# One decoder layer on one core: the feed-forward's way down as a plain product by token quarters, a new order of gate/up, and a new start

## The chip, the cores and the metric

The kernel runs on one core of one Trainium2 chip. The metric is device time in microseconds for one execution; the time of a kernel is the median of its runs. A profiled execution is one more run, recorded by the hardware profiler; its span is what the trace covers.

## The reference

One step of a hybrid decoder, one layer (DEPTH = 1), in fp32. 1024 prompt tokens and 8 x 8 sample tokens share the weights; D_MODEL is 1024 and FFN_HIDDEN 2816. What matters here, cut from the reference:

```python
def rmsnorm(x, g):
    xf = x.astype(jnp.float32)
    y = xf * lax.rsqrt(jnp.mean(xf * xf, axis=-1, keepdims=True) + EPS)
    return (y * g.astype(jnp.float32)).astype(x.dtype)

def swiglu(xn, w_gate, w_up, w_down):
    g = jnp.einsum('btd,df->btf', xn, w_gate)
    u = jnp.einsum('btd,df->btf', xn, w_up)
    return jnp.einsum('btf,fd->btd', jax.nn.silu(g) * u, w_down)

# per layer, for the prompt (yp) and the sample tokens (ys):
#   project_mixers(rmsnorm(yp, g_mix), w_in, ...) -> window attention and mLSTM -> w_out, added to yp
#   yp = yp + cross_attend(rmsnorm(yp, g_cross), ...)
yp = yp + swiglu(rmsnorm(yp, g_ffn[l]), w_gate[l], w_up[l], w_down[l])
ys = ys + swiglu(rmsnorm(ys, g_ffn[l]), w_gate[l], w_up[l], w_down[l])
y_prompt = rmsnorm(yp, g_final)
```

## The kernel before

**Layout and number form.** All 1088 tokens lie as columns, features on the 128 partitions. Every fp32 operand is split into a high and a low part (`split`, and for weights `prep`): a copy to fp32r on ScalarE (ACT) gives the high part, a subtraction on VectorE (DVE) the low one. A product is three matmuls (`mm3`, recorded under line 92): high by high, low by high, high by low. So one weight block of 128 x 128 against one column group makes three matmuls.

**The start.** The x tiles (8 tiles of 128 x 1088) are loaded one after the other on SyncE's queue (SP), split into `xhi` and `xlo` (L116, L117) by ACT or DVE in turn, and squared for the norm (L210). The first two output tiles of the input projection (`win_f[0]`, `win_f[1]`, weights `whi`, `wlo`) run tile by tile as x arrives; their accumulators are `sc`, `o` and `mm`. Then `pt<-sq,ones` sums the squares over the partitions with plain fp32 products, and the products of the token-major weights `win_a` (`wthi`, `wtlo`) follow.

**The feed-forward part** is the last one. Tokens form two halves z of 544 columns; each product has 272 columns. The hidden width is 22 tiles, in 11 pairs `p`. Gate/up (`gate_up`) makes, for each pair and each of the two matrices, a 2 x 2 block product in seven products in place of eight: x is held as `Operand`s (four block pairs, with sums made by `fill`, splits on ACT and DVE, the additions on POOL for z = 0 and on DVE for z = 1), and the weights come as four blocks and four sums of blocks. Each of the seven products of a pair takes one weight `wo` (2 x 512 columns, four blocks of 128) and runs 12 matmuls for each half. Results are combined by `keep` (copy to `kp` on ACT, L1202) and additions and multiplications into `h` on DVE (L1229, L1232, L1233), and `h` is stored to DRAM (`hd`) on POOL's queue.

The first 6 pairs (`NU = 6`) run for z = 0 alone and, much later, for z = 1 alone. Their block sums `sgu` were made ahead of time by DRAM-to-DRAM copies and accumulating copies, spread over earlier parts (`presum`). The last 5 pairs run for both halves together; their block sums `ws` are made by DVE (`sums`, L1131 to L1134). In the same part `dn_sums` makes the block sums of all 11 pairs of down's weights `wdn` on DVE and stores them to DRAM (`sdn`) on POOL's queue.

Down is also a seven-product block product. It goes in six groups of three or four pairs (`downs`), between which the z = 1 runs of pairs 0 to 5 stand (`second`). Each group loads the hidden tiles back from DRAM (`load_h`, `hb<-hd`, 544 KB each) and makes an `Operand` of each. Results are added into `yy` (L1281), which holds the layer's input; `Final` makes squares and their sums, the norm, the last scaling (L1321) and the stores.

**What sets the order.** `all_ops` is the list of all weights in the order of their use; `raw` loads each (`wr`, six buffers) on SP's queue, `prep` splits it (`wo`, five buffers; L1182 on ACT, L1183 on DVE), one weight ahead of its use. A scheduler merges the engines' instructions; on each engine they run in order, so an instruction that waits holds everything behind it on its engine. POOL's queue carries the stores and loads of hidden tiles, of `yy` and of `sdn`. A slot (`slot(tag, ...)`) is reused when its last reader is done.

Of the kernel before, what the change touches and what calls it, by code (L numbers as in the profile page):

```python
# [15 lines left out]
P = 128  # L16
# [9 lines left out]
NU = 6  # L26
# [3 lines left out]
EPS = 1e-6  # L30
NEG = -1.0e30
# [14 lines left out]
def tile_hymba_step(  # L46
# [56 lines left out]

    def gcol(base, k):
        return vv[:, base + k:base + k + 1]


    def split(hi, lo, src, scale=None, eng=None):
# [3 lines left out]
        else:  # L112
            if eng is V:
                V.tensor_scalar_mul(hi, src, scale)
            else:
                A.activation(hi, src, AF.Copy, scale=scale)  # L116
            V.scalar_tensor_tensor(lo, src, scale, hi.bitcast(F32), ALU.mult, ALU.subtract)  # L117

# [75 lines left out]
    xs, xr = [], []  # L194
    for k in range(NK):
        xr.append(slot("cm"[k % 2], [T], name="xraw"))
        nc.sync.dma_start(xr[k], xT[k])
# [4 lines left out]
        if k == 0:  # L202
            w = load_w(win_f[0], NK)
        if k == 0:
            w1 = load_w(win_f[1], NK)
# [56 lines left out]
    def tok_w(src, n, per, tags):  # L262
        parts = []
        for k0 in range(0, NK, per):
            tag = tags[k0 // per]
            raw = wp.tile([P, per, n], F32, tag="wraw", name="wrawt", bufs=2)
            nc.sync.dma_start(raw, src[:, k0:k0 + per, :])
            hi, lo = slot(tag[0], [per, n], F32R, name="wthi"), slot(tag[-1], [per, n], F32R, name="wtlo")
            split(hi, lo, raw)
            parts.append((hi, lo))  # L270
        return lambda k: (parts[k // per][0][:, k % per, :], parts[k // per][1][:, k % per, :])

# [10 lines left out]
    wa = tok_w(win_a, 264, 4, "qm")  # L283
# [12 lines left out]
    for b in range(NB + 1):  # L296
# [4 lines left out]
        if b == NB:  # L301
            next(presum)
# [310 lines left out]
    for blk in range(NB):  # L613
# [25 lines left out]
        if blk % 3 == 1:  # L639
            next(presum)  # L640
# [217 lines left out]
    for u in range(2 * NB):  # L858
# [3 lines left out]
        if u % 3 == 0:  # L862
            next(presum)
# [161 lines left out]
    class Operand:  # L1025
# [14 lines left out]
        def fill(self, b, a, eng=V):  # L1040
            def part(hi, lo, src, scale=None):
# [5 lines left out]
            part(self.b[:, 0:2], self.s_, b)  # L1047
            eng.tensor_tensor(a[:, 0], a[:, 0], a[:, 1], ALU.subtract)
# [6 lines left out]
            return self  # L1055
# [4 lines left out]
    def x_part(z):  # L1060
# [6 lines left out]
        xo[z].append(Operand(xt[z], xo[z][-1] if j % 2 else None).fill(b, a, V if z else G))  # L1067
# [32 lines left out]
    x_part(0)  # L1100
    x_part(0)
# [13 lines left out]
    sdn = dr.tile([NP2, P, 4, 512], F32, name="sdn")  # L1115
# [37 lines left out]
    def dn_ops(g):  # L1153
        for src, i in ((wdn, 0), (wdn, 1), (sdn, 0), (sdn, 1), (sdn, 2), (sdn, 3), (wdn, 3)):
            for p in g:
                yield raw(src[p, :, i, :])


    downs = [(0, (0, 1, 2, 3)), (0, (4, 5, 6, 7)), (0, (8, 9, 10)),
             (1, (7, 8, 9, 10)), (1, (6, 0, 1, 2)), (1, (3, 4, 5))]  # L1160

    second = [(0,), (1,), (2,), (3, 4), (5,), ()]

    def all_ops():
        for p in range(NU):
            yield from gu_ops(p)
        dn = iter(range(NP2))
        for p in range(NU, NP2):
            yield from gu_ops(p)
            for _ in range(3 if p == NP2 - 1 else 2):  # L1170
                dn_sums(next(dn))
        for us, (z, g) in zip(second, downs):
            for p in us:
                yield from gu_ops(p)
            yield from dn_ops(g)
# [335 lines left out]
```

## Time and profile before

| what | us |
|---|---|
| three runs | 1395.67, 1395.81, 1399.73 |
| median | 1395.81 |
| the profiled execution | 1392.54 |
| its span | 1390.70 |
| feed-forward part in it | 604.3 to 1376 |
| TensorE busy | 1288.6 (93%) |
| DVE busy | 939.1 (68%) |
| ACT busy | 684.4 (49%) |
| POOL busy | 187.3 (13%) |

Matmuls are pipelined: a record lasts longer than the distance to the next one, so the cost of a product is read from starts, or from a stretch without gaps. Idle time of an engine other than TensorE costs something only where TensorE waits for that engine.

### The profile page before, as it was taken

Reading aid. Unit: us, or ns where it says so; the run is one execution under the profiler, and the core shown is the slowest. Engines: PE = TensorE matmul, PEld = TensorE weight load, DVE = VectorE, ACT = ScalarE, POOL = GpSimd, SP = SyncE. Lnnn points to the kernel's source line nnn. Section 1 sums busy time; section 2 is a strip of 40 time slices with the busy share of each in tenths; the row PEclk is TensorE's granted clock in tenths of the full one; section 3 lists DMA queues with packets and bytes.
Section 4 is the critical chain, followed back from the end, with each engine's and each line's share of the span. In section 5 each row is a group of like instructions: output and inputs, shape, how many; then the busy total and the mean of one; then the engine's idle time right before and its main releaser. Section 6 shows DMA issues by size and latency. Waiting matters only on the chain.

```text
span 1390.7 us, 24905 instructions
## 1 busy us (share of the span) xinstructions
PE 1288.6 (93%) x9194; PEld 1199.5 (86%) x9194; DVE 939.1 (68%) x2120; ACT 684.4 (49%) x1579; POOL 187.3 (13%) x234
## 2 busy tenths in 40 slices
PE   7999999999999899959999999999798999798996
PEld 6999888887888787759999999999798999798995
DVE  7224345467766677799766665666778798868887
ACT  4322233457654566567654333333555467546553
POOL 2000111200003551350000111112100000200000
PEclk9999999999999999979999999999899999999998
DMA  5123443547763753536764555556756675875663
GB/s 224 38 75 92 145 116 108 135 97 145 241 122 91 197 123 105 176 128 219 241 208 133 184 166 175 166 176 234 248 175 207 188 222 156 289 225 167 200 185 106
DMA packets 108435, 230.44 MB, mean 166 GB/s; under 512 B 13730, under 2 KB 19298, under 8 KB 108314
## 3 DMA queue, kind: packets, MB, share of 16 engines
q1 hardware_dynamic: 82713, 156.50, 36.1%
q0 software_dynamic: 19264, 59.78, 15.8%
q10 hardware_dynamic: 6336, 12.58, 3.0%
q8 instruction: 72, 1.18, 0.4%
q14 instruction: 50, 0.40, 0.1%
HBM read 193.18 MB, written 60.80 MB: 183 GB/s over the span
## 4 chain that ended last, share of the span: by engine, by line
PE 27%; issue 18%; DVE 8%; DMA 4%; POOL 2%; ACT 2%; POOLq 0%; DVEq 0%; SPq 0%; ACTq 0%
PE b L92 25%; POOL sdn L1151 2%; DMA wr<-sgu 1%; DVE wo L1183 1%; DVE bl L111 1%; DVE yy L1321 1%; PE mm L92 1%; DMA wr<-wgu 1%; DMA sdn<-ws 1%; PE sc L92 1%; PE o L92 1%; DMA hb<-hd 0%; DVE bl L117 0%; DVE bs L111 0%; DVE y L1066 0%
## 5 line engine op out<-in xcount | busy, mean ns | idle before, releaser
L92 PE MATMUL b<-bh,wo 128*128 128x272 f32 x2112 | 421.7, 293 | 29.1 <-DVE kp L1232 13.5
L92 PEld LDWEIGHTS b<-bh,wo 128*128 128x128 f32 x2112 | 342.1, 191 | 35.6 <-DVE kp L1232 16.0
L92 PE MATMUL b<-bb,wo 128*128 128x272 f32 x1848 | 322.8, 295 | 23.2 <-DVE wo L1183 10.8
L1183 DVE TENSOR_TENSOR wo<-wr,wo 128x512 fp32r<-128x512 f32 x352 | 238.5, 692 | 105.1 <-ACT wo L1182 105.0
L92 PE MATMUL b<-bl,wo 128*128 128x272 f32 x1056 | 307.7, 291 | 0.0
L1182 ACT ACTIVATE wo<-wr 128x512 fp32r<-128x512 f32 x352 | 218.9, 628 | 169.5 <-PE b L92 117.8
L92 PEld LDWEIGHTS b<-bb,wo 128*128 128x128 f32 x1848 | 277.6, 193 | 27.9 <-DVE wo L1183 12.4
L92 PEld LDWEIGHTS b<-bl,wo 128*128 128x128 f32 x1056 | 201.9, 191 | 0.1
L92 PE MATMUL b<-bs,wo 128*128 128x272 f32 x528 | 153.9, 291 | 0.0
L92 PEld LDWEIGHTS b<-bs,wo 128*128 128x128 f32 x528 | 101.1, 192 | 0.0
L92 PE MATMUL mm<-xlo,whi 128*128 128x384 f32 (+1 forms) x288 | 97.9, 340 | 0.0
L92 PE MATMUL mm<-xhi,whi 128*128 128x384 f32 (+1 forms) x288 | 97.8, 340 | 0.0
L92 PE MATMUL mm<-xhi,wlo 128*128 128x384 f32 (+1 forms) x288 | 96.7, 336 | 0.0
L1202 ACT ACTIVATE kp<-b 128x272 f32<-128x272 f32 x132 | 51.8, 394 | 86.1 <-PE b L92 86.1
L1281 DVE TENSOR_TENSOR yy<-yy,b 128x272 f32<-128x272 f32 x168 | 64.8, 436 | 12.9 <-PE b L92 12.6
L110 ACT ACTIVATE whi<-wraw 128x1024 fp32r<-128x1024 f32 x39 | 41.1, 1055 | 59.5 <-PE mm L92 51.4
L92 PE MATMUL mm<-chi,wlo 128*128 128x384 f32 (+1 forms) x192 | 64.5, 336 | 1.2 <-POOL wlo L111 1.1
L92 PE MATMUL mm<-chi,whi 128*128 128x384 f32 (+1 forms) x192 | 65.2, 340 | 0.0
L92 PE MATMUL mm<-clo,whi 128*128 128x384 f32 (+1 forms) x192 | 63.6, 331 | 0.0
L92 PEld LDWEIGHTS mm<-xhi,whi 128*128 128x128 f32 x288 | 54.8, 190 | 3.1 <-issue 1.8
L92 PEld LDWEIGHTS mm<-xlo,whi 128*128 128x128 f32 x288 | 54.9, 191 | 2.9 <-issue 1.3
L92 PEld LDWEIGHTS mm<-xhi,wlo 128*128 128x128 f32 x288 | 55.0, 191 | 1.5 <-issue 0.9
(390 smaller groups left out, 2242.6 us busy)
## 6 DMA issues: line engine op xcount, KB each, us to landing
wr<-wgu SPq DMA_DIRECT2D x112, 256.0 KB
wr<-wdn SPq DMA_DIRECT2D x110, 256.0 KB
wr<-sgu SPq DMA_DIRECT2D x96, 256.0 KB
wr<-sdn SPq DMA_DIRECT2D x88, 256.0 KB
sgu<-wgu ACTq DMA_DIRECT2D x12, 1024.0 KB
hd<-h POOLq DMA_DIRECT2D x22, 544.0 KB, 4.4
hb<-hd POOLq DMA_DIRECT2D x22, 544.0 KB, 4.8
sdn<-ws POOLq DMA_DIRECT2D x44, 256.0 KB, 5.4
```

Source lines behind the costliest of these rows:

```text
L92: return TE.matmul(out, lhsT, rhs, start=start, stop=stop, skip_group_check=skip)
L110: A.activation(hi, src, AF.Copy)
L111: (eng or V).tensor_tensor(lo, src, hi.bitcast(F32), ALU.subtract)
L1151: G.dma_start(sdn[p, :, i, :], t)
L1182: A.activation(w[:, 0], t, AF.Copy)
L1183: V.tensor_tensor(w[:, 1], t, w[:, 0].bitcast(F32), ALU.subtract)
L1202: A.activation(t, src, AF.Copy)
L1281: V.tensor_tensor(v, v, b[dp], op)
L1321: V.scalar_tensor_tensor(v, v, gcol(V_FIN, 2 * dp + i), r, ALU.mult, ALU.mult)
```

## The change

**The feed-forward part.** `NU` is 4. The order is: pairs 0 to 3 for z = 0 alone, pairs 4 to 10 for both halves, pairs 0 to 3 for z = 1 alone, and then all of down. Down is a plain product, in four token quarters (z, q) of 272 columns: for each of four pairs of output tiles, 22 hidden tiles are accumulated in two banks by 11 weights of 4 blocks, 44 weights a quarter. `wdn` is laid out on the host in this order. No sums of down's weights are made or stored. `hidden` loads the 11 tiles of a quarter from `hd` (272 KB each, in pieces of 1088 bytes, on POOL's queue) into raw slots and splits each once into `hhl`; those of the next quarter are made during the current one. One more weight is prepared ahead (an extra `prep()`). The first two `x_part(0)` calls are cut in two by a `yield`, and the additions of all parts go to DVE. `yy` of z = 1 has slots of its own.

**The start.** Eleven products of a 128 x 128 fp32 tile of zeros with itself go first on TensorE. The first weight and the first x tile are loaded in pieces, the first two weights are split by DVE alone, all x tiles have their high part from ACT. The squares come behind the split of the last x tile, their sums go to DVE alone, and `tok_w(win_a)` is called ahead of the first products.

```diff
-NU = 6
+NU = 4
+IDLE = 11
+    idle = tmp([P], name="idle")
+    V.memset(idle, 0.0)
+    rest = ops([P])
+    for _ in range(IDLE):
+        mm(rest, idle, idle)
...
+    def split_w(raw, parts):
...
+        for k0, k1 in parts:
+            V.tensor_copy(hi[:, k0:k1, :], raw[:, k0:k1, :])
+            V.tensor_tensor(lo[:, k0:k1, :], raw[:, k0:k1, :], hi[:, k0:k1, :].bitcast(F32), ALU.subtract)
...
-        split(hi, lo, xr[k], gcol(V_MIX, k), V if k % 2 else A)
+        if k == 0:
+            raw = first_w(0)
+            nc.sync.dma_start(raw[:, 0:2, :], win_f[0][:, 0:2, :])
+            nc.sync.dma_start(xr[k][:, 0:CH[0][1]], xT[k][:, 0:CH[0][1]])
+            nc.sync.dma_start(xr[k][:, CH[0][1]:T], xT[k][:, CH[0][1]:T])
+            nc.sync.dma_start(raw[:, 2:NK, :], win_f[0][:, 2:NK, :])
+            raw1 = first_w(1)
+            nc.sync.dma_start(raw1, win_f[1])
+            w = split_w(raw, ((0, 2), (2, NK)))
+            for c0, c1 in (CH[0], (CH[0][1], T)):
+                split(hi[:, c0:c1], lo[:, c0:c1], xr[k][:, c0:c1], gcol(V_MIX, k), A)
+            w1 = split_w(raw1, ((0, 2), (2, NK)))
+        else:
+            nc.sync.dma_start(xr[k], xT[k])
+            x_done = split(hi, lo, xr[k], gcol(V_MIX, k), A)
...
-        A.activation(sq, xr[k], AF.Square)
+        with tc.issue_after(x_done.ins):
+            A.activation(sq, xr[k], AF.Square)
...
-            (G if k < 4 else V).tensor_tensor(sums[-1], sums[-1], sq, ALU.add)
+            V.tensor_tensor(sums[-1], sums[-1], sq, ALU.add)
...
+    wa = tok_w(win_a, 264, 4, "qm")
...
-    def dn_sums(p):
-        for i, t in enumerate(sums(*[raw(wdn[p, :, i, :]) for i in range(4)])):
-            G.dma_start(sdn[p, :, i, :], t)
...
     def all_ops():
+        for p in range(NP2):
+            yield from gu_ops(p)
         for p in range(NU):
             yield from gu_ops(p)
...
+        for _ in range(4):
+            for dp in range(4):
+                for i in range(NP2):
+                    yield raw(wdn[dp, i])
...
+    def hidden(z, q):
+
+        hs = [None] * NP2
+
+        def step(p0):
+            n = min(2, NP2 - p0)
+            t = slot("q", [2, 2, HC], name="hraw")
+            for i in range(n):
+                nc.gpsimd.dma_start(t[:, i], hd[z, p0 + i].rearrange("p (a q) c -> p q a c", q=2)[:, q])
+            for i in range(n):
+                o = slot(HT[q][p0 + i], [4, HC], F32R, name="hhl")
+                split(o[:, 0:2], o[:, 2:4], t[:, i])
+                hs[p0 + i] = o
+        return hs, [lambda p0=p0: step(p0) for p0 in range(0, NP2, 2)]
...
+        for dp in range(4):
+            acc = [bank(4 * (dp % 2) + i) for i in range(2)]
+            for i in range(NP2):
                 w = next_w()
+                for j in range(4):
+                    dd, k = divmod(4 * i + j, FT)
+                    o, e = hs[k // 2], k % 2
+                    mm3(acc[dd], w[:, 0, j * P:j * P + P], w[:, 1, j * P:j * P + P],
+                        o[:, e], o[:, 2 + e], k == 0, k == FT - 1)
+                    if k == FT - 1:
+                        v = yy[z][dp][:, dd, q * HC:q * HC + HC]
+                        V.tensor_tensor(v, v, acc[dd], ALU.add)
+                        fin[z].add(2 * dp + dd, q)
...
+    hs, steps = hidden(0, 0)
+    for p in range(NU):
+        gate_up(p, (1,), {1: own if p == 0 else slot("m", [4, HC], name="h")},
+                [lambda: None] * 4 + steps if p == 1 else ())
+    load_yy(1)
...
+    quarters = [(0, 0), (0, 1), (1, 0), (1, 1)]
+    for i, (z, q) in enumerate(quarters):
+        nx_hs, steps = hidden(*quarters[i + 1]) if i < 3 else (None, ())
+        down(z, q, hs, steps)
+        hs = nx_hs
```

TensorE at the program's start; `sc`, `o` are accumulators, `idle` the tile of zeros. Before:

```order
L1507 UNCONDITIONAL_BRANCH
L92 MATMUL sc_171<-xhi_89,whi_95 128x384
L92 MATMUL sc_171<-xlo_90,whi_95 128x384
L92 MATMUL sc_172<-xhi_89,whi_95 128x384
L92 MATMUL sc_171<-xhi_89,wlo_96 128x384
```

And now:

```order
L1514 UNCONDITIONAL_BRANCH
L93 MATMUL o_87<-idle_85 128x128 x11
L93 MATMUL sc_205<-xhi_102,whi_111 128x384
L93 MATMUL sc_205<-xlo_103,whi_111 128x384
L93 MATMUL sc_205<-xhi_102,wlo_112 128x384
```

The eleven zero products stand ahead of the first product with data.

DVE in the part with both halves. Lines 1131 to 1134 of before and 1167 to 1170 of after are block sums of weights: `ws_8945` to `ws_8948` and `ws_8965` to `ws_8968` are sums of `wdn` blocks, `ws_7934` to `ws_7937` of gate/up's blocks. `wo` is a weight's low part, `kp` and `h` belong to the results. Before:

```order
L1183 TENSOR_TENSOR wo_8811<-ws_8772,wo_8811 128x512
L1132 TENSOR_TENSOR ws_8946<-ws_8945,wr_8937 128x512
L1133 TENSOR_TENSOR ws_8947<-wr_8937,wr_8941 128x512
L1183 TENSOR_TENSOR wo_8844<-ws_8774,wo_8844 128x512
L1134 TENSOR_TENSOR ws_8948<-wr_8939,ws_8946 128x512
L1131 TENSOR_TENSOR ws_8965<-wr_8961,wr_8963 128x512
L1132 TENSOR_TENSOR ws_8966<-ws_8965,wr_8957 128x512
L1183 TENSOR_TENSOR wo_8875<-ws_8775,wo_8875 128x512
L1232 TENSOR_TENSOR kp_8754<-b_8770,kp_8754 128x272
```

And now:

```order
L1168 TENSOR_TENSOR ws_7935<-ws_7934,wr_7852 128x512
L1201 TENSOR_TENSOR wo_7757<-ws_7687,wo_7757 128x512
L1169 TENSOR_TENSOR ws_7936<-wr_7852,wr_7856 128x512
L1201 TENSOR_TENSOR wo_7790<-ws_7688,wo_7790 128x512
L1250 TENSOR_TENSOR kp_7708<-b_7724,kp_7708 128x272
L1170 TENSOR_TENSOR ws_7937<-wr_7854,ws_7935 128x512
L1251 SCALAR_TENSOR_TENSOR h_7444<-kp_7708,h_7444 128x272
```

The sums of `wdn` blocks no longer stand among the low parts and results of gate/up; its own sums do.

ACT where the part with both halves ends. `hb` are hidden tiles loaded for a seven-product group, `bb` and `bh` parts of their operands, `hraw` hidden tiles loaded for a quarter, `hhl` their split parts. Before:

```order
L1182 ACTIVATE wo_10595<-wr_10593 128x512
L1182 ACTIVATE wo_10633<-wr_10631 128x512
L110 ACTIVATE bb_10614<-hb_10087 128x272
L110 ACTIVATE bb_10614<-hb_10087 128x544
L1182 ACTIVATE wo_10669<-wr_10667 128x512
L110 ACTIVATE bh_10612<-hb_10087 128x544
L110 ACTIVATE bb_10652<-hb_10130 128x272
```

And now:

```order
L1200 ACTIVATE wo_10797<-wr_10795 128x512
L1200 ACTIVATE wo_10817<-wr_10815 128x512
L117 ACTIVATE hhl_11167<-hraw_11164 128x544
L117 ACTIVATE hhl_11170<-hraw_11164 128x544
L1200 ACTIVATE wo_10836<-wr_10834 128x512
L117 ACTIVATE hhl_11195<-hraw_11192 128x544
L1220 ACTIVATE kp_10812<-b_10794 128x272
L1200 ACTIVATE wo_10856<-wr_10854 128x512
```

Two splits of one raw tile stand between weight copies where four parts of an operand stood.

## Rows read from the trace of the kernel before

**Rows 1.** The page's busy times: engine, us, share of the span, instructions.

```profile
PE 1288.6 (93%) x9194; PEld 1199.5 (86%) x9194; DVE 939.1 (68%) x2120; ACT 684.4 (49%) x1579; POOL 187.3 (13%) x234
```

**Rows 2.** Busy time by stretch, with granted clock, DMA share and GB/s.

```profile
core 0: us, PE busy (x) PEld busy (x) DVE busy (x) ACT busy (x) POOL busy (x), PEclk, DMA share, GB/s
...
613.30:619.00 5.70, 5.63 (x23) 5.42 (x24) 5.70 (x8) 2.67 (x7) 3.43 (x4) 0.51 0.43 139
646.00:755.00 109.00, 109.00 (x868) 108.90 (x869) 79.95 (x152) 63.25 (x133) 4.27 (x8) 1.00 0.66 207
755.00:990.00 235.00, 214.86 (x1661) 211.81 (x1659) 146.46 (x280) 88.14 (x191) 32.87 (x61) 0.97 0.57 184
...
1128.00:1225.00 97.00, 84.51 (x638) 81.13 (x639) 81.30 (x175) 59.23 (x121) 11.61 (x19) 1.00 0.73 238
604.30:1376.00 771.70, 724.42 (x5550) 713.52 (x5550) 580.60 (x1159) 395.32 (x792) 66.47 (x112) 0.97 0.61 193
```

**Rows 3.** TensorE's waits in 604.3 to 1376: us, times, longest.

```profile
PE b L92 <- DVE wo L1183: 13.6, 7, 4.0
PE b L92 <- DVE kp L1232: 13.5, 11, 2.4
PE b L92 <- DVE h L1229: 7.8, 4, 6.5
PE b L92 <- ACT kp L1202: 7.8, 9, 2.4
```

**Rows 4.** Groups by line, 604.3 to 1376: busy us, mean ns, idle before, releasers.

```profile
L1183 DVE TENSOR_TENSOR wo<-wr,wo 128x512 fp32r<-128x512 f32 x352 | 238.5, 692 | 105.1 <-ACT wo L1182 105.0
...
L1131 DVE TENSOR_TENSOR ws<-wr 128x512 f32<-128x512 f32 x21 | 14.5, 692 | 43.7 <-DMA wr<-wdn 26.3 <-DMA wr<-wgu 16.8 <-DVE kp L1232 0.2
...
L1182 ACT ACTIVATE wo<-wr 128x512 fp32r<-128x512 f32 x351 | 218.3, 628 | 169.5 <-PE b L92 117.8 <-DMA wr<-wgu 14.8 <-DMA wr<-sgu 11.0
```

**Rows 5.** Timeline of DVE, then of PE, at one both-halves pair.

```profile
824.90 0.70 DVE L1131 TENSOR_TENSOR ws<-wr 128x512 f32<-128x512 f32 x1 [3.97 <-DMA wr<-wgu]
...
829.01 0.39 PE L92 MATMUL b<-bh,wo 128*128 128x272 f32 x1 [1.60 <-DVE kp L1232]
```

**Rows 6.** Timeline of ACT and PE at the start: start, duration, instruction, idle before.

```profile
5.08 1.20 ACT L116 ACTIVATE xhi<-xraw,vv 128x1088 fp32r<-128x1088 f32 x1 [3.06 <-DMA xraw<-xT]
...
9.72 1.11 ACT L210 ACTIVATE sq<-xraw 128x1088 f32<-128x1088 f32 x1 [0.28 <-DMA xraw<-xT]
...
8.29 0.69 PE L92 MATMUL sc<-xhi,whi 128*128 128x384 f32 x1 [8.29 <-ACT whi L110]
...
12.43 0.52 PE L92 MATMUL mm<-xhi,whi 128*128 128x384 f32 x1
12.75 0.52 PE L92 MATMUL mm<-xlo,whi 128*128 128x384 f32 x1
...
15.44 0.34 PE L92 MATMUL sc<-xhi,whi 128*128 128x384 f32 x1
...
15.96 0.31 PE L92 MATMUL o<-xhi,whi 128*128 128x320 f32 x1
...
37.99 3.82 PE L92 MATMUL pt<-sq,ones 128*128 128x384 f32 x12
```

**Rows 7.** Timeline of PE at the feed-forward's entry and where the both-halves pairs end.

```profile
604.33 0.82 PE L92 MATMUL b<-bb,wo 128*128 128x272 f32 x2 [5.12 <-ACT wo L1182]
...
987.81 0.60 PE L92 MATMUL b<-bh,wo 128*128 128x272 f32 x1 [6.51 <-DVE h L1229]
```

**Rows 8.** DMA issues: queue, count, KB each, median us from issue to landing.

```profile
hb<-hd POOLq DMA_DIRECT2D x22, 544.0 KB, 4.8
...
o_y<-yy POOLq DMA_DIRECT2D x8, 272.0 KB, 3.4
```

**Rows 9.** Timeline of PE and DVE at the end.

```profile
1375.64 0.29 PE L92 MATMUL b<-bh,wo 128*128 128x272 f32 x1
...
1381.46 1.28 PE L92 MATMUL b<-sq,ones 128*128 128x272 f32 x2 [5.53 <-DVE sq L1308]
...
1383.75 3.39 DVE L1321 SCALAR_TENSOR_TENSOR yy<-yy,vv,rf 128x272 f32<-128x272 f32 x8 [2.35 <-ACT rf L163]
```

More of the change, by code (lines that the diff above doesn't have):

```diff
@@ L213, in tile_hymba_step, with tok_w @@
         else:
-            (G if k < 4 else V).tensor_tensor(sums[-1], sums[-1], sq, ALU.add)
+            V.tensor_tensor(sums[-1], sums[-1], sq, ALU.add)
+    def tok_w(src, n, per, tags):
+        parts = []
+        for k0 in range(0, NK, per):
+            tag = tags[k0 // per]
+            raw = wp.tile([P, per, n], F32, tag="wraw", name="wrawt", bufs=2)
+            nc.sync.dma_start(raw, src[:, k0:k0 + per, :])
+            hi, lo = slot(tag[0], [per, n], F32R, name="wthi"), slot(tag[-1], [per, n], F32R, name="wtlo")
+            split(hi, lo, raw)
+            parts.append((hi, lo))
+        return lambda k: (parts[k // per][0][:, k % per, :], parts[k // per][1][:, k % per, :])
+    wa = tok_w(win_a, 264, 4, "qm")
     rstd = slot("r", [T], name="rstd")
@@ L260, in tile_hymba_step @@
         G.memset(mvx[i][:, :, :, P:P + 1], 1.0)
[L262 to L271, printed above, removed]
     def tok_gemm(w, b, n, src=None):
@@ L301, in tile_hymba_step @@
         if b == NB:
-            next(presum)
+            next(presum, None)
     kvf = slot("c", [4, 256], name="kvf")
@@ L639, in tile_hymba_step @@
         if blk % 3 == 1:
-            next(presum)
+            next(presum, None)
     nc.sync.dma_start(o_Cp, CT)
@@ L862, in tile_hymba_step @@
         if u % 3 == 0:
-            next(presum)
+            next(presum, None)
         for _ in range(nfill[u]):
@@ L1255, in gate_up @@
             G.dma_start(hd[z, p], S[z])
-    def load_h(z, p):
-        hb = slot("m", [4, HC], name="hb")
-        G.dma_start(hb, hd[z, p])
-        return hb
     yy = [[None] * 4, [None] * 4]
-    def down(z, hs, done=None, between=()):
-        between = iter(between)
-        n = len(hs)
-        b1 = [bank(i) for i in (1, 2, 6, 7)]
-        def second():
-            return [bank(i) for i in (4, 5, 0, 3)]
-        def product(b, i, start, dd, cc, op=ALU.add, last=False, also=None):
-            for q in range(n):
-                w = next_w()
-                for dp in range(4):
-                    mm3(b[dp], w[:, 0, dp * P:dp * P + P], w[:, 1, dp * P:dp * P + P],
-                        hs[q].hi(i), hs[q].lo(i), start and q == 0, q == n - 1, True)
-                    if q == n - 1:
-                        v = yy[z][dp][:, dd, cc * HC:cc * HC + HC]
-                        V.tensor_tensor(v, v, b[dp], op)
-                        if last and done:
-                            done(2 * dp + dd, cc)
-            for f in between:
-                f()
-                break
-        product(b1, B11, True, 0, 0)
-        product(second(), B21, True, 0, 0, last=True)
-        product(b1, M2, False, 0, 1)
-        b3 = second()
-        product(b3, N1, True, 1, 1, ALU.subtract)
-        product(b1, T3, False, 1, 1, ALU.subtract, last=True)
-        product(b3, B22, False, 0, 1, last=True)
-        product(b1, T4, False, 1, 0, ALU.subtract, last=True)
@@ new lines, in down @@
+    def down(z, q, hs, between=()):
+        between = iter(between)
+        for dp in range(4):
+            acc = [bank(4 * (dp % 2) + i) for i in range(2)]
+            for i in range(NP2):
+                w = next_w()
+                for j in range(4):
[7 more added lines that the diff above has]
+                        fin[z].add(2 * dp + dd, q)
+                if i % 3 == 2:
+                    for f in between:
+                        f()
+                        break
@@ L1335, in tile_hymba_step @@
     prep()
-    x_part(0)
-    x_part(0)
+    rest_of += [x_part(0), x_part(0)]
+    for r_ in rest_of:
+        for _ in r_:
+            pass
+    prep()
     for p in range(NU):
```

86 lines of the change are left out of this document (28 added, 58 removed).

## The prediction

> **What bounds the kernel now.** I read the share of busy time first, then the busy time by stretches, then the waits of TensorE, then single places in the timelines. TensorE is busy 93% of the span [rows 1], so the end is set by how many products it runs, at what pitch, and by the few per cent in which it stands. The profiled execution took 1392.54 us: a span of 1390.70 and 1.84 around it. The median shown is 1395.81, 3.27 above. I sum against 1392.54 and add 3.27 at the end; a difference within 0.3% (4.2 us) cannot be told from no change.
>
> The feed-forward part runs from 604.3 to 1376, 771.7 us [rows 2]. By the code it has 48 x 11 x 7 = 3696 products for gate/up (11 pairs, two halves, two matrices, seven block products of four inner tiles times three) and 6 groups' 1848 for down, 5544 together (the row's 5550 less six sums over partitions). In the stretch 646 to 755, TensorE never stands: 868 products in 109.00 us, 0.1256 us each [rows 2]. So 5544 x 0.1256 = 696.2 us are products and 771.7 - 696.2 = **75.5 us are stalls**. By the same subtraction 755 to 990 loses 235.0 - 1661 x 0.1256 = 26.4 us and 1128 to 1225 loses 97.0 - 80.1 = 16.9. The waits name them: 13.6 us for a weight's low part (`wo`, DVE), 13.5 for `kp` on DVE, 7.8 each for `h` on DVE and `kp` on ACT [rows 3]. These are engines that were held up, not full ones: DVE is busy 580.6 of the 771.7 us [rows 2].
>
> **Products: +33.2 us.** Down as a plain product is 4 quarters x 44 weights x 12 = 2112 products in place of 1848; gate/up keeps its 3696. 5808 - 5544 = 264 more, x 0.1256 = 33.2 us, all on the path. The Trainium skill ("TensorE: Matmul & The Clock Gate", Wait — 56ns, not 53.3ns?) gives columns over 2.4 GHz plus about 2.5 ns, 115.8 ns for 272 columns, and so 30.6 us. The row's 125.6 ns decides.
>
> **Stalls that go: 75.5 us, less what is left.** First the five pairs of both halves (755 to 990). There DVE also sums down's weights, 44 sums, each group behind four loads. The order shows these sums between the sums and the low parts that gate/up waits for. DVE stands 43.7 us at the first sum of a group (`L1131`), 26.3 of it for `wdn` loads and 16.8 for `wgu` loads [rows 4]. What this does to TensorE is in the timeline: at 824.90 DVE had waited 3.97 us at `L1131` for a load, the queue behind it ran off from there, and `kp` came so late that TensorE stood 1.60 us at 829.01 [rows 5]. After, the 44 sums, their 44 loads of four and 44 stores are gone. Two more pairs bring 16 sums of their own (0.69 us each, 11 us [rows 4]); a both-half weight feeds 24 products, 3.0 us, and needs one ACT copy (0.628) and one DVE subtraction (0.692) [rows 4], so they lie under products. I leave about 0.3 us a pair, 2 us.
>
> Next, the six seven-product groups of down. Each reloads its hidden tiles and makes 7 operands of each, in four additions and several splits, and waits for these between products: the stalls from 990 on. A plain quarter needs one split of each tile. Per quarter TensorE has 528 x 0.1256 = 66.3 us. DVE has 44 subtractions (0.692 busy, at most 30.4), 11 splits (about 0.7 each, 8), and 24 small additions (about 0.44, 10): 49 us. ACT has 44 x 0.628 + 11 x 0.7 + 8 x 0.4 = 39 us. Both are covered.
>
> Supply: 44 weights of 256 KB (11.5 MB) and 11 hidden loads of 272 KB (3.06 MB), 14.6 MB in 66.3 us, 220 GB/s. 646 to 755 moved 207 GB/s with no stall, 1128 to 1225 moved 238 with some, 755 to 990 only 184 [rows 2]. I take it that 220 is met, being between the first two; if not, rival C.
>
> **Stalls that stay or come.** (a) The entry of the feed-forward part: TensorE waits 5.12 us for the first weight at 604.33 [rows 7] and runs at a granted clock of 0.51, the lower of its two levels (1.2 GHz), to 619 [rows 2]. After, the four additions of z=0 go from POOL to DVE and a second weight is prepared ahead, but the splits ahead of the first products stay; both stretches up to 646 lose 11.4 us before and I leave 10. (b) The end of the both-half pairs. In the new order ACT's queue has splits of `hraw` between the weight copies; these loads sit in POOL's queue behind the stores of the last pair's hidden tiles. If a load is late, the copies behind it and then TensorE are late. Before has a stall at that place too: 6.51 us at 987.81 [rows 7]. A load of 272 KB takes about 3.4 us to land (`o_y`), one of 544 KB 4.8 [rows 8]. Two weights prepared ahead cover 3.0 us. Bounds 1.5 (the excess of store plus load, 4.8 + 3.4, over what is prepared and not yet used) and 9 (the whole of 4.8 + 3.4 and one split); I take 3.5, near the low end since the store is issued some products earlier. (c) From the last single-half pair to down 1 us and at the three quarter borders 1 us together (0 to 6 each): the next quarter's tiles are loaded during the current one, the sum over partitions is put behind later products by the order, and two accumulators alternate. (d) Lower clock after such waits and the rest: 5.5. Sum 2 + 10 + 3.5 + 2 + 5.5 = **23 us** (12 to 45). The part comes to 33.2 - 75.5 + 23 = **-19.3 us**.
>
> On (b) and (c) a rule speaks against the change: the hidden tiles come in 272 KB where they came in 544. The Trainium skill ("DMA: Bandwidth & Descriptors", Bandwidth) wants transfers of 1 MiB and more, and its fit (Anatomy of one DMA) gives about 2.6 us for 272 KB and 3.3 for 544. The trace's 3.4 and 4.8 are longer in both, so by the page (b) would be some 1.5 us less; I stay with the rows.
>
> **Start: -8 us.** Now the first product starts at 8.29 and the products show the lower level: 0.32 us from start to start for 384 columns (12.43, 12.75), against 0.17 at the upper one later (three in 0.52 us, 15.44 to 15.96) [rows 6]. The first x tile is split at 5.08, the second lands at 9.72, and the phase ends at 37.99 [rows 6]. After, 11 zero products of 128 fp32 columns go first. The row of 12 fp32 products (2176 columns by the code) took 3.82 us at the upper level [rows 6], 1.755 ns a column: 11 x 128 columns take 2.5 us, or 4.9 at the lower level, ending at about 6 us. The first products (tile and weight in pieces) then start near 6.5, and from the second x tile, 9.72 plus a split of 1.2, at 10.9, the clock should be at the upper level. Seven x tiles of two weights, 1088 columns and three products, at 0.173/384 us a column, are 7 x 2.94 = 20.6: the phase ends near 31.5, 6.5 earlier. Up to 2.9 us more lie in the next 11 us (waits for token weights whose load now goes first; some lower clock). Bounds 4 and 10; I take 8. The squares move behind the last x split and their sums from POOL to DVE; the products cover them. In exchange, if x tiles land late (split by ACT alone, 1.2 us each), nothing is lost: tiles come every 1.5 to 3 us.
>
> **Weight sums at the start and middle: 0.** Four of the twelve 1-MB copies and four accumulating ones go, in queues that nothing waits for before 604 (-2 to 0).
>
> **Tail: -4 us.** Before: last product 1375.64, then four additions, squares, sums, one partition sum of two (1.28 us) at 1381.46, eight scalings (3.39 us) from 1383.75, the store, end 1390.70 [rows 9]: 15.1 us. After, the last step closes one output tile, not four: product 0.29, addition 0.44, square 0.43, sum 0.44, partition sum 1.28, root 0.98, scalings 3.39 and the last store 3.5 make 10.8. Gain 4 (2 to 5).
>
> **Sum.** 1392.5 - 8 - 19.3 - 4 = 1361.2 for a profiled execution; + 3.3 gives **1364 us**.
>
> **Rivals.** A (forecast), 1364. B, late hidden tiles: loads are issued when TensorE is already at the border, so each of the five borders (end of the pairs, start of down, three between quarters) costs a landing (3.4) and a split (1.3): 23.5 us where I have 5.5: 1364 + 18 = **1382**. For it: POOL's queue is in order and the raw slots are few; against: only two tiles are needed to start. C, down bound by its supply: if a quarter gets 184 GB/s (the row of 755 to 990), 14.6 MB take 79.3 us instead of 66.3, 4 x 13 = 52 more: **1416**, slower. It decides from 197 GB/s (74.1 us a quarter) down. For it: loads in short pieces beside the weights; against: 1128 to 1225 moved 238 [rows 2]. D, the zeros do nothing (the clock is at its lower level again when the first products come, or the x loads bind): start gain 0, **1372**.
>
> **How the numbers follow.** A 0.66, B 0.14, C 0.10, D 0.10. Slower by over 0.3% (above 1400): most of C, 0.08. Within 0.3%: 0.04, from the ends of B and C. Faster: 0.88. The range: low end A with start -10, tail -5 and stalls of 12: 1364 - 2 - 1 - 11 = 1350, less 4 for executions that lie nearer the profiled one: 1346. High end: B with the start at its weak bound: 1382 + 6 = 1388. C is left out.
>
> **What would show it.** Clock at the upper level by 9 us and the x phase ending before 33: start right. Both-half pairs with under 1 us of waits each: the DVE queue was the cause. Down quarters at 66 to 68 us each and over 215 GB/s: C wrong; 75 or more with waits for `wr`: C right. Waits on `hhl` at borders above 4 us: B. A pitch above 0.13 us in down with no wait named would make the sum itself wrong.

## The result, and the profile after

The changed kernel takes 1356.95 us in the median of four runs (1353.73 to 1363.44), before 1395.74 beside it: a ratio of 0.972, 95% interval 0.968 to 0.977. The forecast was 1364, range 1346 to 1388. The profiled execution took 1353.75 with a span of 1352.0; the sum had said 1361.2 for it. Runs of one kernel differ by some 10 us, and in 160 to 300 us, ahead of the feed-forward part, the granted clock was between 0.94 and 1.00 in the traces of this study, so small edits below are judged by stretches of the traces and not by whole times.

The busy times, as in [rows 1]:

```profile
PE 1299.1 (96%) x9480; PEld 1217.8 (90%) x9480; DVE 820.3 (61%) x1819; ACT 658.5 (49%) x1507; POOL 153.4 (11%) x189
```

The waits of TensorE over the whole span (us in total, times, longest):

```profile
PE b L93 <- DVE wo L1201: 8.1, 2, 7.9
PE b L93 <- ACT kp L1220: 6.0, 3, 3.5
PE b L93 <- DVE rf L1127: 3.8, 1, 3.8
PE b L93 <- ACT wo L1200: 3.1, 2, 2.6
```

Against [rows 3] the waits for `kp` on DVE are gone, those for `h` on DVE are down to 0.7 us, and those for `wo` are one long wait of 7.9 us. The stretches, to be read beside [rows 2]: the entry; the seven pairs with both halves (688.20 to 983.20; 740 to 989 is the stretch that expectations below speak of); the z = 1 pairs, which begin behind them; and the four quarters of down, from 1074.50 on:

```profile
588.00:634.00 46.00, 34.92 (x241) 33.40 (x242) 43.54 (x92) 32.44 (x66) 1.07 (x2) 0.84 0.47 146
...
688.20:983.20 295.00, 295.00 (x2355) 295.00 (x2354) 157.62 (x292) 111.74 (x239) 9.65 (x17) 1.00 0.24 78
...
740.00:989.00 249.00, 246.26 (x1965) 246.04 (x1963) 130.82 (x242) 93.18 (x199) 10.75 (x18) 1.00 0.25 81
...
983.20:1074.40 91.20, 85.20 (x673) 84.25 (x672) 59.87 (x106) 54.39 (x110) 13.24 (x21) 1.00 0.77 248
...
1074.50:1141.80 67.30, 66.49 (x530) 65.83 (x529) 45.66 (x77) 38.93 (x70) 12.89 (x20) 1.00 0.80 257
1141.80:1208.80 67.00, 66.37 (x532) 66.07 (x531) 44.72 (x78) 36.24 (x65) 10.63 (x15) 1.00 0.75 234
1208.80:1275.40 66.60, 66.46 (x532) 66.16 (x531) 42.44 (x74) 32.84 (x58) 2.87 (x4) 1.00 0.70 200
1275.40:1341.70 66.30, 66.30 (x532) 66.05 (x530) 36.55 (x64) 28.77 (x50) 0.00 (x0) 1.00 0.55 160
```

In the pairs TensorE does not stand at all, and DVE is busy 53% of the time (157.62 of 295.00 us) where it was 62% (146.46 of 235.00). The 249 - 1965 x 0.1256 = 2.2 us that 740 to 989 seems to lose are the start of a wait that ends at 989.72, behind the pairs. Down runs at 0.126 to 0.127 us a product, while 257 GB/s move in its first quarter and 160 in its last. The group of all 2112 products of down shows the same in one line (busy us, mean ns, idle before them):

```profile
L93 PE MATMUL b<-hhl,wo 128*128 128x272 f32 x2112 | 264.8, 287 | 0.8 <-ACT wo L1200 0.5
```

The two profiled spans differ by 38.7 us, and the trace divides this at the first feed-forward product (588.01 after, 604.33 before) and the last (1341.6 and 1375.64):

| stretch | before | after | measured | forecast |
|---|---|---|---|---|
| to the first feed-forward product | 604.3 | 588.0 | -16.3 | -8 |
| feed-forward products and stalls | 771.3 | 753.6 | -17.7 | -19.3 |
| last product to the end | 15.1 | 10.4 | -4.7 | -4 |

### The profile page after: what moved, and what is told of

It reads as the page before. It is cut to its first block, busy times and chain, and to the rows that moved or that the text cites. A ratio compares the mean times of both kernels' runs of the same rounds, so it can differ in the third digit from the quotient of the medians.

```text
span 1352.0 us, 24812 instructions
## 1 busy us (share of the span) xinstructions
PE 1299.1 (96%) x9480; PEld 1217.8 (90%) x9480; DVE 820.3 (61%) x1819; ACT 658.5 (49%) x1507; POOL 153.4 (11%) x189
## 4 chain that ended last, share of the span: by engine, by line
PE 51%; DVE 4%; DMA 3%; ACT 2%; issue 2%; POOL 0%; DVEq 0%; ACTq 0%; POOLq 0%
PE b L93 49%; DMA hraw<-hd 3%; PE mm L93 1%; PE o L93 1%; ACT wo L1200 1%; DMA wr<-wgu 1%; PE sc L93 1%; DVE wo L1201 0%; DVE nb L943 0%; DVE bl L118 0%; DVE yy L1340 0%; DVE rf L1127 0%; ACT hhl L117 0%; ACT sp L964 0%; DVE y L1100 0%
## 5 line engine op out<-in xcount | busy, mean ns | idle before, releaser
L93 PE MATMUL b<-bh,wo 128*128 128x272 f32 x1408 | 276.1, 289 | 8.8 <-ACT kp L1220 6.0
L93 PE MATMUL b<-hhl,wo 128*128 128x272 f32 x2112 | 264.8, 287 | 0.8 <-ACT wo L1200 0.5
L93 PEld LDWEIGHTS b<-hhl,wo 128*128 128x128 f32 x2112 | 263.4, 188 | 1.7 <-ACT wo L1200 0.7
L93 PEld LDWEIGHTS b<-bh,wo 128*128 128x128 f32 x1408 | 225.0, 188 | 10.6 <-ACT kp L1220 7.0
L93 PE MATMUL b<-bb,wo 128*128 128x272 f32 x1232 | 211.7, 291 | 10.5 <-DVE wo L1201 7.9
L93 PE MATMUL b<-bl,wo 128*128 128x272 f32 x704 | 202.8, 288 | 0.4 <-DVE bl L124 0.4
L93 PEld LDWEIGHTS b<-bb,wo 128*128 128x128 f32 x1232 | 182.8, 190 | 11.4 <-DVE wo L1201 8.3
L93 PEld LDWEIGHTS b<-bl,wo 128*128 128x128 f32 x704 | 132.7, 188 | 0.6 <-DVE bl L124 0.6
L93 PE MATMUL b<-bs,wo 128*128 128x272 f32 x352 | 101.8, 289 | 0.0
L1201 DVE TENSOR_TENSOR wo<-ws,wo 128x512 fp32r<-128x512 f32 x56 | 38.7, 691 | 42.6 <-ACT wo L1200 42.6
```

The lines of the kernel that those rows point to most:

```text
L93: return TE.matmul(out, lhsT, rhs, start=start, stop=stop, skip_group_check=skip)
L1201: V.tensor_tensor(w[:, 1], t, w[:, 0].bitcast(F32), ALU.subtract)
```

## The experiments

Where a trace is said to be ahead of or behind another by so many us at some place, that is the difference of the starts of one and the same product in the two.

**The changed kernel again**, the yardstick.

> The changed kernel again, as it is: the yardstick for the runs beside it. Both theories: 1353 to 1363 us, about 0.972 of before. If its runs differ among themselves by 7 us as in the first comparison (1353.7 and 1363.4), its trace and clocks should say in which stretch: the granted clock over the span would be 0.988 in the short runs and 0.98 in the long ones.

Measured 1355.97 (1354.5 to 1363.86), ratio 0.973 (0.969 to 0.978). It repeats the result. The mean granted clock was 0.976 in the run of 1363.86 and 0.983 to 0.986 in the other three, in the direction expected; the trace is of the run of 1355.98, so where the longest loses was not seen.

**The new start alone**, in the kernel before (`NU = 6`, everything from the feed-forward part as before).

> The kernel before with the new start alone (zeros first, loads in pieces, token weights ahead, squares behind); the feed-forward part and its sums are untouched. Between the two traces the lead grew from 8.3 us at 84 us of the span to 13.5 at the first partition sum ahead of the feed-forward part. Theory: all of that lead is the start's, since the instructions between are the same, and a shifted start changes which waits fall together: 1382 to 1384. Rival: the lead beyond 8.3 us comes from the four copies and four accumulating copies that the changed kernel no longer makes: 1387 to 1388, with ACT's split ahead of 475 us still late by some 5 us.

Measured 1385.61 (1380.15 to 1388.76), ratio 0.993 (0.990 to 0.996), between the two, and 9.2 us under the kernel before beside it (1394.77). The trace decides for the rival in one place: the wait for `qhl` stays, 5.00 us at 471.58.

**Down's sums left out of the kernel before**:

```diff
-            for _ in range(3 if p == NP2 - 1 else 2):
-                dn_sums(next(dn))
...
-        for src, i in ((wdn, 0), (wdn, 1), (sdn, 0), (sdn, 1), (sdn, 2), (sdn, 3), (wdn, 3)):
+        for src, i in ((wdn, 0), (wdn, 1), (wdn, 0), (wdn, 1), (wdn, 2), (wdn, 3), (wdn, 3)):
```

> The kernel before without the sums of down's weights (their 44 loads, 44 sums and 44 stores are left out; the groups of down read plain blocks where they read sums, the same number of loads and products). Theory: the stalls of the five pairs with both halves (26.4 us of 755 to 990) come from DVE standing at these sums for their loads; without them that stretch loses 2 to 4 us and the kernel takes 1370 to 1375. Down as seven products then still loses its 36 us from 990 on. Rival: these pairs wait because one weight ahead is too few, or for the results themselves, whatever stands between: at least 15 us of the 26 stay and the kernel takes 1383 or more.

Measured 1376.99 (1372.26 to 1381.69), ratio 0.987 (0.983 to 0.991). In its trace the products of 755 to 990 (757.8 to 973.6 here) take 215.8 us in place of 235:

```profile
757.80:973.60 215.80, 208.79 (x1660) 208.18 (x1659) 122.36 (x237) 88.89 (x191) 9.04 (x17) 0.99 0.28 94
```

215.8 - 1660 x 0.1256 = 7.3 us are left of 26.4, and 7.1 of them are the two waits at the end of the pairs (5.50 and 1.58). **The sums cost this stretch 19 us**, nearly all that was lost in the pairs, and down as seven products kept its own stalls. What is left, and the time, are above what was expected (2 to 4 us, 1370 to 1375), because the stretch takes in the end of the pairs; in the pairs themselves no wait is left, with one weight ahead, so the rival is out.

**The sums put back**, as dead work, into the changed kernel, whole and in their parts:

```diff
+    def dn_sums(p):
+        for i, t in enumerate(sums(*[raw(wdn[dp, p]) for dp in range(4)])):
+            G.dma_start(sdn[p, :, i, :], t)
...
             yield from gu_ops(p)
+            if p >= NU:
+                for _ in range(2):
+                    for q in dn:
+                        dn_sums(q)
+                        break
```

> The changed kernel with the sums of down's weights put back as dead work between the pairs with both halves (44 loads, 44 sums on DVE, 44 stores, two groups after each pair until all eleven are made; nothing reads them). In the changed kernel TensorE loses about 2 us in 740 to 989. Theory: DVE stands at these sums for their loads again and TensorE behind it: 12 to 20 us more in that part, 1366 to 1376 in all, with waits for kp on DVE. Rival: the second weight prepared ahead now covers them: under 4 us more.

> The changed kernel with the 44 dead loads of down's blocks alone in the places of dn_full, no sums and no stores. If the loads themselves (their share of the six raw buffers and of SP's queue) make the weights late: 6 us or more in that part, with waits for wo. If what costs is that DVE waits for them in its queue: under 3 us more.

> The changed kernel with 44 dead sums on DVE that read blocks already on chip (eleven groups of gate/up's sums are made twice), no loads and no stores. They add 44 x 0.6 = 27 us of DVE time to a part of 249 us in which DVE is busy 131. If DVE's time is what costs: 5 us or more in that part. If it is the wait for loads: under 2 us more.

> The changed kernel with the dead sums of dn_full and with one weight prepared ahead in place of two. With two ahead the dead sums cost 8.6 us in 740 to 989, where the five pairs of before gave back 19.3 when their sums were left out. Theory: the second weight ahead hides the rest: with one ahead the part loses 15 us or more against the changed kernel. Rival: the difference comes from spreading the sums over more pairs: 8 to 10 us as with two. At the end of the pairs one weight less ahead should make the waits behind the hidden tiles' splits longer by 1.5 to 3 us.

One row of the stretches of each, over the same 2458 products of the pairs; the changed kernel, dn_full, dn_loads, dn_resident and dn_full_one in this order:

```profile
672.10:980.00 307.90, 307.90 (x2458) 307.90 (x2457) 167.64 (x309) 119.54 (x256) 7.88 (x15) 1.00 0.25 82
```

```profile
678.10:994.50 316.40, 310.78 (x2456) 309.49 (x2455) 191.03 (x353) 119.46 (x256) 31.52 (x59) 0.99 0.47 152
```

```profile
673.70:981.60 307.90, 307.90 (x2458) 307.90 (x2457) 167.45 (x309) 119.37 (x256) 7.89 (x15) 1.00 0.37 119
```

```profile
673.90:981.80 307.90, 307.90 (x2458) 307.90 (x2457) 193.91 (x353) 119.80 (x256) 7.89 (x15) 1.00 0.25 82
```

```profile
675.00:998.40 323.40, 313.69 (x2458) 312.40 (x2457) 191.42 (x353) 119.28 (x256) 31.74 (x59) 0.98 0.47 149
```

The 44 loads alone cost nothing, 44 sums on DVE alone (26 us more of DVE) cost nothing, and together, with the stores, they cost 8.5 us with two weights ahead and 15.5 with one (one weight ahead by itself costs these pairs nothing, as the sums left out of the kernel before showed). The whole times, one run each, were 1367.34, 1357.4, 1358.27 and 1372.37. For dn_full I had expected 12 to 20; the second weight ahead hides almost half, as the run with one weight shows. The longer waits at the end of the pairs that I had expected with one weight did not come: those for `kp` on ACT there are 4.9 us in both runs with the sums and 6.0 in the changed kernel. How the loss comes about stands in dn_full's timeline of DVE, and of TensorE behind it:

```profile
813.20 0.68 DVE L1170 TENSOR_TENSOR ws<-wr,ws 128x512 f32<-128x512 f32 x1
817.91 0.69 DVE L1167 TENSOR_TENSOR ws<-wr 128x512 f32<-128x512 f32 x1 [4.03 <-DMA wr<-wgu]
818.52 0.69 DVE L1213 TENSOR_TENSOR wo<-wr,wo 128x512 fp32r<-128x512 f32 x1
...
822.18 0.43 DVE L1262 TENSOR_TENSOR kp<-b,kp 128x272 f32<-128x272 f32 x1
...
822.67 0.39 PE L93 MATMUL b<-bh,wo 128*128 128x272 f32 x1 [2.32 <-DVE kp L1262]
```

It is the picture of [rows 5] again: DVE stands 4.03 us at the first sum for its loads, and `kp`, which is ready to be added, waits in the queue behind. The stores were not tried alone, and dead loads free their buffers as soon as they land, while sums hold them; so the runs show that the loads must have a waiting sum behind them, not which of buffer and queue counts more.

**The copies for pairs 4 and 5 back**:

```diff
-        groups = [sums_of(a, a + 2) for a in range(0, NU, 2)]
+        groups = [sums_of(a, a + 2) for a in range(0, NU + 2, 2)]
```

> The changed kernel with the DRAM copies and accumulating copies of six pairs in place of four, as before had them (the sums of pairs 4 and 5 are made and not read). In the three traces with six pairs TensorE waits 4.8 to 5.0 us for ACT's split of the cross queries (qhl) near 475 us, in the three with four pairs 0.2 to 0.6. Theory: the copies delay the loads of the output weights, the weight's split waits for its load and qhl stands behind it on ACT: the wait is 4 to 5 us again, and the kernel some 4 us longer in that stretch. Rival: the wait has to do with the start or the order of other work: it stays under 1 us.

Measured 1372.6 in its one run; of this the granted clock of 0.94 in 160 to 300 explains a part that has nothing to do with the edit. The wait for `qhl`, TensorE's timeline before, after, and with the copies:

```profile
475.37 1.04 PE L92 MATMUL sc<-kvhl,qhl 64*128 64x256 f32 x6 [4.87 <-ACT qhl L110]
```

```profile
463.69 1.08 PE L93 MATMUL sc<-kvhl,qhl 64*128 64x256 f32 x10 [0.24 <-ACT qhl L117]
```

```profile
479.00 1.26 PE L93 MATMUL sc<-kvhl,qhl 64*128 64x256 f32 x8 [4.83 <-ACT qhl L117]
```

and ACT's timeline with the copies:

```profile
463.68 0.50 ACTq L189 DMA_DIRECT2D sgu<-wgu  x1
...
474.14 1.06 ACT L117 ACTIVATE whi<-wraw 128x1024 fp32r<-128x1024 f32 x1 [5.16 <-DMA wraw<-wout]
...
478.54 0.42 ACT L117 ACTIVATE qhl<-xq 128x256 fp32r<-128x256 f32 x1 [1.45 <-DVE xq L935]
```

A 1-MB copy goes out at 463.68; ACT stands 5.16 us for a weight's load, and `qhl` is behind it. The load was issued at 465.23 and split 8.9 us later; in the changed kernel the load of the same weight was issued at 454.52 and split 4.0 us later. From 30 products before this wait to 200 behind it, the kernel before takes 44.82 us, the changed kernel 39.41 and the changed kernel with the copies 44.84: **the copies cost 5.4 us here**, where some 4 were expected. The theory of the expectation holds; whether the plain copies or the accumulating ones do it was not tried. In the trace of before the same wait of ACT, at 470.50, is put down to TensorE's `mm`, which ends at nearly the same moment; the run with the copies is what names the load. What moved in 420 to 490, with the copies and in the changed kernel:

```profile
420.00:490.00 70.00, 61.20 (x363) 55.84 (x362) 43.85 (x74) 34.31 (x73) 30.45 (x19) 0.98 0.55 144
```

```profile
420.00:490.00 70.00, 67.00 (x399) 61.15 (x400) 48.83 (x76) 38.01 (x80) 35.64 (x22) 0.99 0.27 84
```

**The zeros left out** (`IDLE = 0`).

> The changed kernel without the eleven zero products. Theory: the first products of data run at the lower clock; 18 of them take 0.32 us in place of 0.17, 2.6 us, of which 1.4 lie in the waits that TensorE has there anyway (0.9 at 9.2 us and 0.5 at 11.5): 1 to 3 us more than the changed kernel beside it. Rival: the zeros do nothing, the x tiles set the end of the phase: within 0.7 us of it.

Measured 1359.79 (1353.96 to 1369.82), ratio 0.975 (0.970 to 0.981): the times tell nothing apart from the changed kernel. In the traces the sum of squares, the end of the x phase, starts at 34.83 without the zeros, at 33.81 and 32.97 in the two traces of the changed kernel: 1.0 to 1.9 us, as expected. But the other nine traces of this study with the same new start put it at 33.09 to 34.99, so the eleven with zeros reach from 32.97 to 34.99 and the one without lies among them: **that the zeros gain anything is not shown**. The first products ran at the lower clock without them and not with them (0.32 and 0.18 us from start to start), but in both TensorE then stands at `mm` until DVE has split the second weight (1.15 us without the zeros, 0.89 with them in the trace shown, up to 2.47 in the others). No_zeros, then the changed kernel, where each of the eleven fp32 products leaves two records:

```profile
10.12 0.69 PE L93 MATMUL mm<-xhi,whi 128*128 128x384 f32 x1 [1.15 <-DVE whi L214]
10.61 0.52 PE L93 MATMUL mm<-xlo,whi 128*128 128x384 f32 x1
10.93 0.52 PE L93 MATMUL mm<-xhi,whi 128*128 128x384 f32 x1
```

```profile
1.21 4.54 PE L93 MATMUL o<-idle 128*128 128x128 f32 x22 [1.21 <-DVE idle L106]
5.50 0.42 PE L93 MATMUL sc<-xhi,whi 128*128 128x384 f32 x1
...
9.23 0.44 PE L93 MATMUL mm<-xhi,whi 128*128 128x384 f32 x1 [0.89 <-DVE whi L214]
9.51 0.34 PE L93 MATMUL mm<-xlo,whi 128*128 128x384 f32 x1
9.69 0.34 PE L93 MATMUL mm<-xhi,whi 128*128 128x384 f32 x1
...
32.97 3.82 PE L93 MATMUL pt<-sq,ones 128*128 128x384 f32 x12
```

**The second weight earlier** (the second `prep()` moved up behind the first).

> The changed kernel with the second weight of the feed-forward part prepared before the rest of the x operands and not after it. In the changed kernel TensorE waits 7.9 us at 602.8 for that weight's low part, which stands on DVE behind some 30 instructions of the operands. Theory: the second product's twelve matmuls then run inside that wait (12 x 0.227 at the lower clock, 2.7 us); the third product still needs the last operand's low part, which DVE finishes at 601.7 as before, so 2 to 3 us are won and not 8. Rival: DVE's total is what counts, and the wait only moves: under 1 us.

Measured 1354.62 in one run. Against the changed kernel it is 1.7 us behind at the first product (589.71) and 0.9 at the 240th (634.77): 0.8 won, so the rival holds and not the theory. (The 1.8 us that the last expectation below names set against each other products that stand in another order in the two.) From the first to the 240th product it takes 45.1 us, the eight traces with this entry unchanged 45.2 to 45.9. The wait of 7.7 us is still there, one weight later and again for `wo`: DVE is full, and the next weight's low part stands behind the operands as the second's did.

**The first quarter's splits later**, as a bunch, each ordered behind a result's copy on ACT:

```diff
+    def behind(f):
+        with tc.issue_after(mark[0].ins):
+            f()
...
-            A.activation(t, src, AF.Copy)
+            mark[0] = A.activation(t, src, AF.Copy)
...
-                [lambda: None] * 4 + steps if p == 1 else ())
+                [lambda: None] * 4 + [lambda f=f: behind(f) for f in steps] if p == 1 else ())
```

> The changed kernel with the splits of the first quarter's hidden tiles on ACT ordered behind a copy of a result of the second pair of the last part (z = 1 alone), some 25 us later; the loads stay. In the changed kernel TensorE waits 3.5, 1.2 and 1.4 us for kp on ACT between 989 and 1007, where ACT stands at splits whose load has not landed. Theory: these three waits go (under 1 us left), 4 to 6 us won in that part and nothing lost later, since down begins 60 us after. Rival: the copies on ACT are late for another reason (ACT is busy or results come late): 3 us or more stay.

Measured 1357.88 in one run. The three waits went: from 5.5 us behind at 953 the trace is 1.8 ahead at 1007. But it is 3.8 behind at 1145. "Nothing lost later" was wrong. From the last product of the pairs with both halves to the first of down's second quarter it takes 157.5 us; the changed kernel takes 158.8 in its first trace and 164.9 in the trace of its second series, so what the edit wins in sum is not settled. ACT's timeline where the bunch now stands, and TensorE's:

```profile
1026.72 0.66 ACT L117 ACTIVATE hhl<-hraw 128x544 fp32r<-128x544 f32 x1 [1.97 <-DMA hraw<-hd]
1027.29 0.61 ACT L1200 ACTIVATE wo<-wr 128x512 fp32r<-128x512 f32 x1
1028.35 0.66 ACT L117 ACTIVATE hhl<-hraw 128x544 fp32r<-128x544 f32 x1 [0.45 <-DMA hraw<-hd]
1028.92 0.38 ACT L1225 ACTIVATE kp<-b 128x272 f32<-128x272 f32 x1
...
1029.35 0.40 PE L93 MATMUL b<-bh,wo 128*128 128x272 f32 x1 [2.19 <-ACT kp L1225]
```

The raw slots are few, so a load can go out only when a split has freed its slot, and the next split of the bunch waits for it, with `kp` behind.

**The splits spread out, and two edits at the entry** (the splits in pairs behind every fifth product of the last three pairs; the second weight earlier; the additions of z = 0 back on POOL):

```diff
-        steps = o.fill(b, a)
+        steps = o.fill(b, a, V if z else G)
...
+    spread = iter([x for f in steps for x in [lambda: None] * 4 + [lambda f=f: behind(f)]])
...
-                [lambda: None] * 4 + steps if p == 1 else ())
+                spread if p else ())
```

> The changed kernel with three edits at two places. At the entry of the feed-forward part: the second weight is prepared ahead of the rest of the operands (1.8 us won in prep_early), and the four additions of the z = 0 operands go back from DVE to POOL. At the end of the pairs: the splits of the first quarter's hidden tiles are spread, one load's worth behind every fifth product of the last three single-half pairs, each behind a copy of a result on ACT. Theory: bunched 25 us later they won 7.2 us and gave back 5.5 where they came together; spread, each finds its load landed and nothing stands behind it: 6 to 7 us won from 985 to 1095 and under 1.5 given back. From the partition sum to the steady products it was 18.2 us after and 15.2 before, with POOL's additions: with both edits 13 to 15, so 3 to 5 us won. In all 8 to 11 us, 1343 to 1348 for a run as short as the changed kernel's shortest, about 1347 in the median. Rival: POOL is slower at the additions and the splits still stand before copies: under 3 us in all.

Measured 1349.72 in the median of six (1346.91 to 1353.52), ratio 0.971 (0.967 to 0.974). That is 41 us faster than the kernel before beside it; against the changed kernel the ratios' intervals overlap, and the trace has to tell. At the end of the pairs it gains 7.2 us (from 2.1 ahead at 965 to 9.3 at 1047) and gives back 2.1 by 1145: **5.1 won**, within the 4.5 to 7 that the expectation makes, though more was given back than the 1.5 allowed. By the measure used for the last edit it is 153.6 us, under all six traces in which this part is unchanged (158.8 to 164.9). At the entry it gains nothing (2.5 ahead at 564, 2.0 at 634) where I had expected 3 to 5, so in all it is 5 us and not 8 to 11. DVE's timeline shows why:

```profile
589.31 1.28 DVE L1100 SCALAR_TENSOR_TENSOR y<-y,vv,rf 128x544 f32<-128x544 f32 x1
590.51 2.42 DVE L1201 TENSOR_TENSOR wo<-wr,wo 128x512 fp32r<-128x512 f32 x2
...
594.42 1.28 DVE L118 TENSOR_TENSOR bl<-y,bh 128x544 fp32r<-128x544 f32 x1
```

While POOL adds (1.1 us each), a subtraction of 512 columns takes DVE 1.2 us and one of 544 columns 1.28, where they take 0.69 and 0.72 alone.

## Why the prediction was right, and where it was off

**Products, +33.2 us: right.** All 5808 run at about the pitch of before; the quarters' partition sums start at 1144.99, 1211.51, 1277.38 and 1343.37, 66.5, 65.9 and 66.0 us apart, against 66.3 forecast. Supply held (257 GB/s in the first quarter, in 66.49 of whose 67.30 us TensorE was busy), so rival C is refuted. Its row of 184 GB/s was what that stretch had asked for while TensorE stood, not what the transfers could give, as the 257 show.

**Stalls, 75.5 to 23: right in sum, 753.6 - 5808 x 0.1256 = 24.1.** By place: the pairs nothing (forecast 2), and the sums left out and put back show that what they had lost was DVE's wait for loads; the entry 15.7 (10); the end of the pairs 6.0 in its three waits (3.5); borders and the rest about 2.4 (7.5). The entry and the end of the pairs were put too small, the rest too large, and that the sum fits is luck. At the entry I had seen the additions go from POOL to DVE and costed them at nothing, but DVE was full there (43.54 of 46.00 us), and the second weight's low part stood behind them: the wait of 7.92 at 602.84. That the additions alone made DVE full is not shown: with them back on POOL, DVE's other work took longer and nothing was won. The first product starts 3.3 us behind the partition sum in place of 6.2, which gave back 2.9 of this; I put that down to the yield, which was not tried alone. In sum the stretch from the partition sum to the 240th product took 49.2 us, 47.8 before.

```profile
584.69 0.72 PE L93 MATMUL b<-rf,ones 128*128 128x272 f32 x2 [3.84 <-DVE rf L1127]
588.01 1.12 PE L93 MATMUL b<-bb,wo 128*128 128x272 f32 x3 [2.60 <-ACT wo L1200]
...
602.84 0.82 PE L93 MATMUL b<-bb,wo 128*128 128x272 f32 x2 [7.92 <-DVE wo L1201]
```

**The end of the pairs: mechanism right, size too small.** Its three waits take 6.0 us where I had put 3.5, inside the bounds of 1.5 and 9. The timelines of ACT and TensorE there show it as forecast, a split that waits for its load, `kp` behind it, TensorE behind `kp`; the two runs on the splits show that this is the cause:

```profile
988.72 0.66 ACT L117 ACTIVATE hhl<-hraw 128x544 fp32r<-128x544 f32 x1 [3.77 <-DMA hraw<-hd]
989.28 0.38 ACT L1220 ACTIVATE kp<-b 128x272 f32<-128x272 f32 x1
...
989.72 0.39 PE L93 MATMUL b<-bh,wo 128*128 128x272 f32 x1 [3.45 <-ACT kp L1220]
```

Rival B, the same at each border, did not come: waits of 0.6 us and less. The hidden loads took 5.3 us to land in the median. The 3.4 that I had assumed for them is the row of a store (`o_y<-yy`), not of a load, but outside this place nothing needs them early. The comparison with the Trainium skill ("DMA: Bandwidth & Descriptors", Anatomy of one DMA) was summed wrongly, too: by the estimates from its fit, 3.3 and 2.6 us, the store and the load come to 5.9 in place of 8.2, 2.3 less and not 1.5.

**Start, -8: right in sum (8.2 at the token products, 51.00 before and 42.77 after), split wrongly.** The x phase ended 5.0 us earlier, not 6.5, and the waits behind it gave 3.2. The sign that I had named, an end before 33, is met by this trace alone (32.97) of the eleven with the new start and its zeros, so the 5.0 is its best case; by the medians the new start alone is worth 9.2 us. That the zeros have a part in it is not shown, and the loads in pieces, the splits that changed engine and the token weights ahead were not tried one by one. Rival D (start gain absent) is out, but its reason, zeros that do nothing, is not.

**Weight sums, 0: the step that failed.** I put the copies in queues that nothing waits for. Nothing waits for them, but a load beside them, for which ACT waits, was late with them at 475 us, and TensorE waited behind ACT: 4.87 us before, 0.24 after, 4.83 with the copies back. It cost 5.4 us with all that hung on it. With this and the earlier first product (2.9) the -16.3 of the table is 8.2 + 5.4 + 2.9, and 0.2 too much.

**Tail, -4: right**, 10.4 us after the last product in place of 15.1.

So, by this account, the time that was won did not come from down as such: 33 us of products more against 32 of other stalls less (75.5 - 24.1 - 19) is about even. What it brought is that its weights need no sums (19 us, in and right behind the pairs), that fewer copies run (5), a shorter tail (5), and the start (8).

## What to carry to other kernels

An algorithm that saves products must be charged with what prepares its operands, at the place where that work stands in a queue: here one product in eight was saved, and the sums that it needed stopped the engine that every other product depended on. Work that waits for a load must not stand ahead of work that does not, and it has to be spread so that each load has landed; moving it in a bunch moves the wait. A transfer that nobody waits for can still make another one late.

## What the runs showed of the hardware

A VectorE subtraction of 512 columns took 1.2 us beside GpSimd's additions and 0.69 without them (spread, 590.51, and [rows 4]), so VectorE, relieved of work by GpSimd, may lose as much as it gains. The Trainium skill ("SBUF — State Buffer", Who interferes with whom) says that a VectorE instruction with two SBUF inputs contends with a GpSimd instruction that reads SBUF, and that the ports they share are an exclusive lock, which would make such an instruction wait while one of the other's runs; the row agrees with it (0.5 us more, under one addition of 1.1). And copies from DRAM to DRAM on ACT's queue, with accumulating ones on POOL's, made a load on SP's queue some 5 us late at 144 GB/s in that stretch, far below the 257 of down's first quarter, so it was not the rate in sum that ran out; what held the load is open.
